# Where the first weight split of the next step stands in the vector queue of a fused encoder block on Trainium2

## The chip, the cores and the metric

The kernel is one program on one core of one Trainium2 chip. Its time is device microseconds (us) from one execution; the time before is the median of three runs. All five engines of the core take part: TensorE (PE) multiplies, ScalarE (ACT) rounds and evaluates functions, VectorE (DVE) subtracts, adds and multiplies, GpSimd (POOL) and SyncE (SP) mostly issue transfers. Each engine works through its own queue in the order in which the program was built.

## The reference

One encoder block on 256 tokens of width 4096, all in float32. Cut to its matrix products:

```python
h = rms_norm(x, pre_norm_gain)
proj = h @ w_in                      # 4096 x 24,704 columns
(q, k, v, gate_a, qi, ki, wi, z, xs, bm, cm, dt_raw, merge_logits) = split(proj)
y_a = dsa_attention(rope(q), rope(k), v, rope(qi), rope(ki), wi * s) * silu(gate_a)
y_b = ssd_mixer(xs, z, bm, cm, dt_raw, ...)
merged = (sigmoid(merge_logits)[0] * (y_a @ w_branch_attn)
          + sigmoid(merge_logits)[1] * (y_b @ w_branch_ssd))
out = merged @ w_out
return x + rms_norm(out, post_norm_gain)
```

The products with `w_in`, the two branch matrices and `w_out` are nearly all of the work. The attention (top 64 keys by an indexer, softmax) and the state-space scan are small beside them.

## The kernel before

**Precision.** A float32 operand is used as a sum of two parts: a rounded one ("h", fp32r) and the remainder ("l"). A product a·b is three matmuls, l(a)·h(b), h(a)·l(b) and h(a)·h(b), into one bank of PSUM. For the activations (256 tokens, kept in SBUF as `base` and as sums and differences `ext`) the two parts are made once. The weights are streamed from HBM and split as they arrive: `split` (line 483) takes one tile of two 128x512 blocks, lets ScalarE round it into a tile `wh` (line 486), and lets VectorE subtract to get the remainder `wl` (line 490, or line 488 where the sign is turned). Below, "rounding" and "remainder" mean these two instructions, and "a split" means both. In a matmul the activation part is the loaded weight matrix and the `wh` or `wl` block streams through.

**Two kinds of step.** Most products go through `pair_gemm` (line 515). It makes 256 tokens x 1024 columns at a time. Its loop runs over 16 pairs of row blocks of the weights (`plan`); each pair is a 2x2 block product and is one step. A step of kind S has 7 block products instead of 8, that is 21 matmuls, and pays with extra sums of weight blocks on VectorE (lines 598 and 599). A step of kind D or R has 8 block products, 24 matmuls. The program has 172 steps of kind S and 276 of kinds D and R, and every S step here is followed by a step of kind D or R.

**What a step of kind S puts on the engines**, in the order of the code (lines 593 to 605, kind "S"): the split of the second raw tile `rb`, the split of the first raw tile `ra`, the subtraction of line 598 in `ra`, the subtraction of line 599 in `rb`, the split of one block of `ra` (128x512, called t2 below), and the split of `rb` (t3 and t4, the last split of the step). Then its seven products in the order 2, 5, 3, 1, 6, 7, 4. The remainder of the last split is first read by the second matmul of product 7, which is matmul 17 of the 21. A step of kind D or R has two splits: first `ra` with the sign turned (rounding on line 486, remainder on line 488), read by its first 12 matmuls, then `rb`, read by its other 12.

**Buffers.** The rounded tiles lie in a pool of `SBUFS = 5` buffers, the remainders in another five. In both programs the first rounding of a step that follows an S step goes into the buffer of the last rounding before that S step, that is of the tile `rb` of the step ahead of it. It can be written when the last matmul of that earlier step has read it. Raw tiles have 8 buffers and are fetched two steps ahead (`LEAD = 2`).

**Order.** The program is written against a framework that reorders each engine's instructions by its own estimate of when each is ready, keeps the dependences, and adds the waits. Between the matmuls of a step, `step()` lets pending work (rotary embedding, softmax, the scan, evacuation of results) put out some instructions of its own; this is called side work below.

Of the kernel before, what the change touches and what calls it, by code (L numbers as in the profile page):

```python
# [19 lines left out]
S = 256  # L20
# [26 lines left out]
def fused_block(tc, x, xT, w_qi, w_misc, w_q0, w_qk, w_vg, w_x, w_z, w_gate, w_br, w_out2, w_out,  # L47
# [24 lines left out]
    def fbit(ap):  # L72
        return ap.bitcast(F32)
# [406 lines left out]
        k = int(name[2]) - 1  # L480
        return base[i][:, 0, k, tk], base[i][:, 1, k, tk]

    def split(src, n, sign=1):
        h = whp.tile([P, n, NW], F32R, tag="wh", name="wh")
        l = wlp.tile([P, n, NW], F32R, tag="wl", name="wl")
        A.activation(h, src, AF.Copy, scale=float(sign))  # L486
        if sign < 0:
            V.scalar_tensor_tensor(l, src, -1.0, fbit(h), ALU.mult, ALU.subtract)  # L488
        else:
            V.tensor_sub(l, src, fbit(h))  # L490
        return [(h[:, j, :], l[:, j, :]) for j in range(n)]
# [23 lines left out]
    def pair_gemm(what, mode, chunk, plan, outs, evac, hooks={}, pace=1):  # L515

        while len(live) > 1:
            drain(live.popleft())
        left = {}
        for _, kind in plan:  # L520
            for j, n in USES[kind].items():
                left[j] = left.get(j, 0) + n
        ps = {}
        dest = []

        def product(j, i, name, w):
            (ah, al), (bh, bl) = form(i, name), w
            first = j not in ps
            if first:
                ps[j] = bank(phys[j])  # L530
            left[j] -= 1
            for n, (l, r) in enumerate(((al, bh), (ah, bl), (ah, bh))):
                T.matmul(ps[j], l, r, start=first and n == 0, stop=left[j] == 0 and n == 2)  # L533

        def early():
            dest.extend(outs())
            A.activation(dest[0], ps[1], AF.Copy)
            V.tensor_add(dest[1], ps[6], dest[0])
            V.tensor_add(dest[2], ps[7], dest[1])

        def late():
            if not dest:
                dest.extend(outs())
                A.activation(dest[1], ps[5], AF.Copy, scale=-1.0)
                return
            V.tensor_add(dest[1], ps[5], dest[1])
            if 8 in ended:
                V.tensor_sub(dest[3], dest[3], ps[5])  # L548
                return
            V.scalar_tensor_tensor(dest[3], ps[5], -1.0, dest[2], ALU.mult, ALU.subtract)  # L550

        def rest():
            c11, c12, c21, c22 = dest
            if 1 not in ps:
                A.activation(c11, ps[2], AF.Copy)
                A.activation(c21, ps[4], AF.Copy)
                V.tensor_sub(c22, c12, ps[8])
                V.tensor_sub(c12, c12, ps[3])
                return
            V.scalar_tensor_tensor(c12, ps[3], -1.0, c12, ALU.mult, ALU.subtract)  # L560
            if 8 in ps and 8 not in ended:
                V.tensor_sub(c22, c22, ps[8])
            V.tensor_add(c11, ps[2], c11)
            V.tensor_add(c21, ps[4], c21)

        def end():
            rest()
            live.append(push(evac(dest)))

        after = max([n for n, (_, kind) in enumerate(plan) if kind == "S"], default=-2) + 1  # L570
        ended = []
        loaded = deque()

        def fetch(n):
            i, kind = plan[n]
            ra, rb = raw_tile(), raw_tile()
            load_half(ra, chunk(i), 0)
            load_half(rb, chunk(i), 1)
            if kind == "S":
                nc.gpsimd.dma_start(ra[:, 0, :], chunk(i)[:, HK, :], accum_op=ALU.add)  # L580
            loaded.append((ra, rb))

        for n in range(LEAD):
            fetch(n)
        for n, (i, kind) in enumerate(plan):
            if n + LEAD < len(plan):
                fetch(n + LEAD)
            ra, rb = loaded.popleft()
            if n in hooks:
                hooks[n]()  # L590
            assert kind_of[i] == what, (n, i, kind_of, len(aux))
            assert kind == "R" or ext_n[i] == {"S": 4, "D": 2}[kind], (n, i, ext_n)
            if kind == "S":
                b11, b21 = split(rb, 2)
                t1, b22 = split(ra, 2)
                if n == 1:
                    run_pending()
                V.tensor_sub(ra[:, 1, :], ra[:, 0, :], ra[:, 1, :])  # L598
                V.tensor_sub(rb, rb, ra[:, 1:2, :].to_broadcast([P, 2, NW]))  # L599
                t2, = split(ra[:, 1:2, :], 1)  # L600
                t3, t4 = split(rb, 2)
                now = {1: ("A11", b11), 2: ("A12", b21), 3: ("S4", b22), 4: ("A22", t4),
                       5: ("S1", t1), 6: ("S2", t2), 7: ("S3", t3)}
                for j in (2, 5, 3, 1, 6, 7, 4):
                    product(j, i, *now[j])
            else:
                w = {}
                w[1, 2], w[2, 2] = split(ra, 2, -1)
                w[1, 1], w[2, 1] = split(rb, 2)
                if n == 0 and len(pending) > 1 and turned[0] == "aux":  # L610
                    pending.pop(0)()
                if n == 1:
                    run_pending()
                if n == after:
                    early()
                    if not left.get(5):
                        late()
                        ended.append(5)
                if n == len(plan) - 1 and dest and not ended and left.get(8) == 0:
                    V.scalar_tensor_tensor(dest[3], dest[2], -1.0, ps[8], ALU.mult, ALU.subtract)  # L620
                    ended.append(8)
                todo = [(k, j) for j in ((5, 3, 2, 4) if kind == "D" else (3, 8, 2, 4))
                        for k in (1, 2)]
                for k, j in todo:
                    name = {2: f"A1{k}", 4: f"A2{k}", 8: f"A2{k}", 5: f"A2{k}",
                            3: f"D{k}" if kind == "D" else f"A1{k}"}[j]
                    product(j, i, name, w[k, 1 if j in (2, 4) else 2])
                    if (k, j) == todo[3]:
                        step(pace)
            step(pace)  # L630
        if 5 not in ended:
            pending.append(late)
        pending.append(end)
        turn(mode)
# [388 lines left out]
    for g, cols in enumerate(GATES):  # L1023
        last = g == len(GATES) - 1
        plan = kinds(SX if g > 1 else SS, range(16), range(8, 16) if last else ())
# [71 lines left out]
    for n in range(0, 8, 2):  # L1097
        for br in range(2):
            pairs = range(8 * br, 8 * br + 8)
            plain = pairs if (n, br) in ((0, 0), (6, 1)) else ()  # L1100
            plan = kinds(SY, pairs, plain)
# [47 lines left out]
    for n in range(0, 6, 2):  # L1149
# [5 lines left out]
        plan = [(i, "R" if k == "D" else k) for i, k in kinds(SM, order, plain)]  # L1155
# [65 lines left out]
    def finish_tok(t, ps):  # L1221
        with tc.high_priority():
# [7 lines left out]
         plan=[(h, (0, 1)) for h in range(12)]  # L1230
# [102 lines left out]
```

## Time and profile before

| | before |
|---|---|
| median of three runs | 2837.47 us (2835.63 to 2841.07) |
| the profiled execution | 2835.93 us |
| its span, first to last instruction | 2833.8 us |
| TensorE busy, matmuls | 2808.8 us (99%), 12744 |
| VectorE busy | 2318.9 us (82%) |
| ScalarE busy | 1693.3 us (60%) |
| mean granted TensorE clock | 0.998 |
| HBM traffic | 224 GB/s over the span |

In a row of the timeline view stand the start, the duration, the engine, the line of the kernel, the operation, its tiles written as out<-in (buffer numbers left out), the shape, how many equal instructions were merged into the row, and in brackets the idle time before it and what ended that. `b` and `ext` are activation parts, `p` and `pc` results. A matmul row with `wh` streams a rounded weight block, one with `wl` a remainder. The shown duration of a matmul is longer than its distance to the next one, since they overlap in the array. In the waits view a row has the total, the count and the longest wait in us. In a row of the groups view stand after the bar the busy time, the mean ns of one, and the idle time before.

### The profile page before, as it was taken

What the parts mean: (1) busy time and instruction counts of PE and PEld (TensorE: products, weight loads), DVE (VectorE), ACT (ScalarE), POOL (GpSimd) and SP (SyncE); (2) the same over time, 40 slices, a digit from 0 to 9 for tenths busy, and PEclk for the clock granted to TensorE, in tenths of its full rate; (3) what the DMA queues carried; (4) which work ended last, traced back from release to release, by engine and by line L of the source; (5) the groups of instructions that cost most, each with busy time, mean ns of one, the idle gap of its engine ahead of it and who ended that gap; (6) DMA issues with size and microseconds to landing.
All of it is one profiled execution on the core that took longest, in us unless ns stands there. A gap on an engine that the chain in (4) does not pass through costs nothing.

```text
span 2833.8 us, 36254 instructions
## 1 busy us (share of the span) xinstructions
PE 2808.8 (99%) x12744; PEld 2314.6 (82%) x12744; DVE 2318.9 (82%) x2867; ACT 1693.3 (60%) x2210; POOL 179.8 (6%) x216
## 2 busy tenths in 40 slices
PE   9999999999999999999999999999999999999998
PEld 7877888888888888888888888888887888888886
DVE  6668988888888878888888888888887889878875
ACT  7444565565656656886678755555565545555553
POOL 0100000000000000000000000000000000000000
PEclk9999999999999999999999999999999999999999
DMA  9544776777767776666666877877777887877883
GB/s 373 192 159 165 214 222 202 226 212 222 223 200 224 212 220 217 195 201 207 209 192 195 256 245 242 247 231 244 236 242 243 245 259 242 284 226 227 257 259 134
DMA packets 198696, 637.54 MB, mean 225 GB/s; under 512 B 22385, under 2 KB 23153, under 8 KB 198513
## 3 DMA queue, kind: packets, MB, share of 16 engines
q1 hardware_dynamic: 163728, 567.05, 59.8%
q0 software_dynamic: 27008, 52.44, 10.5%
q10 hardware_dynamic: 7776, 15.73, 1.5%
q8 instruction: 100, 1.64, 0.2%
q14 instruction: 84, 0.68, 0.1%
HBM read 615.21 MB, written 19.92 MB: 224 GB/s over the span
## 4 chain that ended last, share of the span: by engine, by line
PE 89%; DVE 5%; issue 3%; DMA 2%; ACT 1%; SPq 0%; POOL 0%; DVEq 0%; ACTq 0%; POOLq 0%
PE p L533 74%; PE p L193 4%; PE p L194 4%; PE p L195 4%; DVE wl L490 1%; PE p L363 1%; ACT wh L486 1%; DMA fr<-yscr 1%; PE p L890 0%; DVE raw L599 0%; DMA raw<-w_x_d 0%; DVE wl L185 0%; PE p L758 0%; PE p L725 0%; PE p L394 0%
## 5 line engine op out<-in xcount | busy, mean ns | idle before, releaser
L486 ACT ACTIVATE wh<-raw 128x1024 fp32r<-128x1024 f32 (+1 forms) x1240 | 1190.9, 995 | 775.3 <-PE p L533 443.0
L533 PE MATMUL p<-wh,b 128*128 128x512 f32 x4504 | 1511.9, 393 | 3.5 <-DVE pc L548 1.9
L490 DVE TENSOR_TENSOR wl<-raw,wh 128x1024 fp32r<-128x1024 f32 (+1 forms) x964 | 1064.1, 1125 | 242.8 <-ACT wh L486 237.7
L533 PEld LDWEIGHTS p<-wh,b 128*128 128x128 f32 x4504 | 846.5, 188 | 179.3 <-ACT wh L486 4.4
L533 PE MATMUL p<-wl,b 128*128 128x512 f32 x2252 | 878.8, 390 | 1.6 <-DVE wl L490 0.9
L533 PE MATMUL p<-wh,ext 128*128 128x512 f32 x2320 | 810.4, 390 | 0.0
L533 PEld LDWEIGHTS p<-wh,ext 128*128 128x128 f32 x2320 | 435.5, 188 | 91.2 <-ACT wh L486 0.9
L533 PEld LDWEIGHTS p<-wl,b 128*128 128x128 f32 x2252 | 423.5, 188 | 88.2 <-DVE wl L488 2.7
L533 PE MATMUL p<-wl,ext 128*128 128x512 f32 x1160 | 452.6, 390 | 0.6 <-DVE wl L490 0.2
L488 DVE SCALAR_TENSOR_TENSOR wl<-raw,wh 128x1024 fp32r<-128x1024 f32 x276 | 337.0, 1221 | 86.5 <-ACT wh L486 82.5
L533 PEld LDWEIGHTS p<-wl,ext 128*128 128x128 f32 x1160 | 217.8, 188 | 48.5 <-DVE wl L490 2.8
L599 DVE TENSOR_TENSOR raw<-raw 128x1024 f32<-128x1024 f32 x172 | 210.5, 1224 | 4.2
L185 DVE TENSOR_TENSOR wl<-raw,wh 128x1024 fp32r<-128x1024 f32 x112 | 138.7, 1240 | 84.4 <-ACT wh L184 84.3
L193 PE MATMUL p<-wh,b 128*128 128x512 f32 x512 | 201.4, 394 | 1.4 <-ACT wh L181 1.4
L194 PE MATMUL p<-wl,b 128*128 128x512 f32 x512 | 199.6, 390 | 0.2 <-DVE wl L182 0.2
L195 PE MATMUL p<-wh,b 128*128 128x512 f32 x512 | 199.3, 389 | 0.0
L184 ACT ACTIVATE wh<-raw 128x1024 fp32r<-128x1024 f32 x112 | 118.2, 1059 | 130.3 <-PE p L195 117.0
L598 DVE TENSOR_TENSOR raw<-raw 128x512 f32<-128x512 f32 x172 | 118.6, 689 | 3.8
L193 PEld LDWEIGHTS p<-wh,b 128*128 128x128 f32 x512 | 96.0, 188 | 25.9 <-ACT wh L181 3.4
L194 PEld LDWEIGHTS p<-wl,b 128*128 128x128 f32 x512 | 96.2, 188 | 20.2 <-DVE wl L182 1.0
L195 PEld LDWEIGHTS p<-wh,b 128*128 128x128 f32 x512 | 96.1, 188 | 20.1
L580 POOL DMA_DIRECT2D raw<-w_gate_d x50 | 43.3, 867 | 587.5 <-DMA raw<-w_gate_d 280.2
(238 smaller groups left out, 1443.4 us busy)
## 6 DMA issues: line engine op xcount, KB each, us to landing
raw<-w_gate_d SPq DMA_DIRECT2D x256, 512.0 KB, 5.1
raw<-w_vg_d SPq DMA_DIRECT2D x128, 512.0 KB, 4.8
raw<-w_x_d SPq DMA_DIRECT2D x128, 512.0 KB, 4.7
raw<-w_br_d SPq DMA_DIRECT2D x128, 512.0 KB, 4.8
raw<-w_out_d SPq DMA_DIRECT2D x128, 512.0 KB, 4.8
raw<-w_qk_d SPq DMA_DIRECT2D x96, 512.0 KB, 4.7
raw<-w_z_d SPq DMA_DIRECT2D x64, 512.0 KB, 4.8
raw<-w_qi_d SPq DMA_DIRECT2D x62, 512.0 KB, 5.5
```

Of the source, the lines that this page charges most:

```text
L184: A.activation(wh, rs, AF.Copy)
L185: V.tensor_sub(wl, rs, wh.bitcast(F32))
L193: T.matmul(ps[t], al[:, tk], wh[:, i, :], start=first, stop=False)
L194: T.matmul(ps[t], ah[:, tk], wl[:, i, :], start=False, stop=False)
L195: T.matmul(ps[t], ah[:, tk], wh[:, i, :], start=False, stop=last)
L486: A.activation(h, src, AF.Copy, scale=float(sign))
L488: V.scalar_tensor_tensor(l, src, -1.0, fbit(h), ALU.mult, ALU.subtract)
L490: V.tensor_sub(l, src, fbit(h))
L533: T.matmul(ps[j], l, r, start=first and n == 0, stop=left[j] == 0 and n == 2)
L580: nc.gpsimd.dma_start(ra[:, 0, :], chunk(i)[:, HK, :], accum_op=ALU.add)
L598: V.tensor_sub(ra[:, 1, :], ra[:, 0, :], ra[:, 1, :])
L599: V.tensor_sub(rb, rb, ra[:, 1:2, :].to_broadcast([P, 2, NW]))
```

## The change

`split` gets a function `between`, which it calls after it has put out the rounding and before it puts out the remainder. The first split of a step is moved into `head(n)`. The last split of an S step calls `head(n + 1)` in between; in a step that does not follow an S step, `head(n)` is called at the start of the step. No instruction is added or dropped by this; the first split of a step after an S step is built earlier, and the last remainder of the S step is built after both its instructions.

```diff
-    def split(src, n, sign=1):
+    def split(src, n, sign=1, between=None):
         h = whp.tile([P, n, NW], F32R, tag="wh", name="wh")
         l = wlp.tile([P, n, NW], F32R, tag="wl", name="wl")
         A.activation(h, src, AF.Copy, scale=float(sign))
+        if between is not None:
+            between()
         if sign < 0:
             V.scalar_tensor_tensor(l, src, -1.0, fbit(h), ALU.mult, ALU.subtract)
         else:
...
+        heads = {}
+
+        def head(n):
+            if n < len(plan) and n not in heads:
+                ra, rb = loaded[0]
+                heads[n] = split(rb, 2) if plan[n][1] == "S" else split(ra, 2, -1)
+
...
         for n, (i, kind) in enumerate(plan):
             if n + LEAD < len(plan):
                 fetch(n + LEAD)
+            head(n)
             ra, rb = loaded.popleft()
...
             if kind == "S":
-                b11, b21 = split(rb, 2)
+                b11, b21 = heads[n]
                 t1, b22 = split(ra, 2)
...
                 t2, = split(ra[:, 1:2, :], 1)
-                t3, t4 = split(rb, 2)
+                t3, t4 = split(rb, 2, between=lambda: head(n + 1))
...
             else:
                 w = {}
-                w[1, 2], w[2, 2] = split(ra, 2, -1)
+                w[1, 2], w[2, 2] = heads[n]
                 w[1, 1], w[2, 1] = split(rb, 2)
```

A line of the old program stands two to ten lines lower in the new one: the remainders are on lines 488 and 490 before and on 490 and 492 after, the matmul on 533 and 535, the two subtractions on 598 and 599 and on 608 and 609.

VectorE's queue of the program before, in the S step at 1707 us of the profiled execution. The tile wl_14860 is the remainder of t2, wl_14864 that of the last split of the step, wl_14889 the first and wl_14893 the second remainder of the step that follows.

```order
L598 TENSOR_TENSOR raw_14769<-raw_14769 128x512
L599 TENSOR_TENSOR raw_14770<-raw_14770,raw_14769 128x1024
L490 TENSOR_TENSOR wl_14860<-raw_14769,wh_14859 128x512
L490 TENSOR_TENSOR wl_14864<-raw_14770,wh_14863 128x1024
L488 SCALAR_TENSOR_TENSOR wl_14889<-raw_14813,wh_14888 128x1024
L490 TENSOR_TENSOR wl_14893<-raw_14814,wh_14892 128x1024
```

The same place in the changed program; the first remainder of the following step is now wl_14867.

```order
L608 TENSOR_TENSOR raw_14769<-raw_14769 128x512
L609 TENSOR_TENSOR raw_14770<-raw_14770,raw_14769 128x1024
L492 TENSOR_TENSOR wl_14860<-raw_14769,wh_14859 128x512
L490 SCALAR_TENSOR_TENSOR wl_14867<-raw_14817,wh_14866 128x1024
L492 TENSOR_TENSOR wl_14864<-raw_14770,wh_14863 128x1024
L492 TENSOR_TENSOR wl_14893<-raw_14818,wh_14892 128x1024
```

The two remainders have changed places: the following step's first one stands ahead of the S step's last one. It is so in all 172 S steps. ScalarE's queue has the three roundings in the same order in both programs.

On TensorE the framework keeps the order of the matmuls around most S steps and changes it around some. The next piece is from before, in the S step at 1724 us; wh_15000 and wl_15001 are its last split (products 7 and 4), wh_15036 and wl_15037 the first split of the step after it.

```order
L533 MATMUL p4_15021<-wh_15000,ext_2525 128x512
L533 MATMUL p4_15021<-wl_15001,ext_2525 128x512
L533 MATMUL p4_15021<-wh_15000,ext_2525 128x512
L533 MATMUL p6_14969<-wh_15000,b1_79 128x512
L533 MATMUL p6_14969<-wl_15001,b1_79 128x512
L533 MATMUL p6_14969<-wh_15000,b1_79 128x512
L533 MATMUL p1_14948<-wh_15036,b2_80 128x512
L533 MATMUL p1_14948<-wl_15037,b2_80 128x512
L533 MATMUL p1_14948<-wh_15036,b2_80 128x512 x2
```

The same place in the changed program, where the step's last split is still wh_15000 and wl_15001 and the following one is wh_15003 and wl_15004.

```order
L535 MATMUL p4_15025<-wh_15000,ext_2525 128x512
L535 MATMUL p6_14969<-wh_15000,b1_79 128x512
L535 MATMUL p1_14948<-wh_15003,b2_80 128x512
L535 MATMUL p1_14948<-wl_15004,b2_80 128x512
L535 MATMUL p1_14948<-wh_15003,b2_80 128x512 x2
L535 MATMUL p4_15025<-wl_15001,ext_2525 128x512
L535 MATMUL p4_15025<-wh_15000,ext_2525 128x512
L535 MATMUL p6_14969<-wl_15001,b1_79 128x512
L535 MATMUL p6_14969<-wh_15000,b1_79 128x512
```

Here five matmuls that do not need wl_15001 have been moved ahead of the first one that does. Counted over the program, the first reader of an S step's last remainder is matmul 17 of the step in 162 of 172 S steps before and in 108 after; in the other 64 between one and nineteen other matmuls stand ahead of it. GpSimd's queue is unchanged, and in SyncE's some weight loads and loads of the gates have changed places by a few positions.

## The prediction

> **What bounds the kernel now.** I read the page first: who is busy, and who is on the chain that ended last.
>
> ```profile
> PE 2808.8 (99%) x12744; PEld 2314.6 (82%) x12744; DVE 2318.9 (82%) x2867; ACT 1693.3 (60%) x2210; POOL 179.8 (6%) x216
> PE 89%; DVE 5%; issue 3%; DMA 2%; ACT 1%; SPq 0%; POOL 0%; DVEq 0%; ACTq 0%; POOLq 0%
> ```
>
> TensorE is busy throughout and carries 89% of the chain. Next come the waits: first those of TensorE in the pair products, then the largest of ScalarE.
>
> ```profile
> PE p L533 <- ACT wh L486: 1.6, 5, 0.5
> PE p L533 <- DVE wl L490: 1.2, 2, 0.9
> PE p L533 <- DVE wl L488: 0.5, 1, 0.5
> ACT wh L486 <- PE p L533: 443.0, 358, 2.6
> ```
>
> TensorE waits for splits 3.3 us in all (1.6 + 1.2 + 0.5), while ScalarE waits for TensorE to free buffers 358 times. The splits run ahead of the matmuls and are held back by the five buffers. So the change can gain hardly anything, and the question is whether it lets a remainder come too late. For that I read the timeline of one ordinary S step, engine by engine. TensorE:
>
> ```profile
> 1706.77 0.39 PE L533 MATMUL p<-wh,b 128*128 128x512 f32 x1
> ...
> 1709.27 0.62 PE L533 MATMUL p<-wh,b 128*128 128x512 f32 x2
> ...
> 1712.66 0.62 PE L533 MATMUL p<-wh,ext 128*128 128x512 f32 x2
> 1713.12 0.39 PE L533 MATMUL p<-wl,ext 128*128 128x512 f32 x1
> 1713.35 0.39 PE L533 MATMUL p<-wh,ext 128*128 128x512 f32 x1
> ```
>
> At 1706.77 the earlier step begins the 12 matmuls on its second split. The first of the two in the row at 1709.27 is the twelfth, the other begins the S step. The row at 1713.12 is matmul 17 of the S step, the first reader of its last remainder. From 1706.77 to 1713.12 are 28 matmuls, 0.227 us each: nothing waits. ScalarE and then VectorE in the same step:
>
> ```profile
> 1707.01 0.63 ACT L486 ACTIVATE wh<-raw 128x512 fp32r<-128x512 f32 x1 [2.48 <-PE p L533]
> 1708.27 1.06 ACT L486 ACTIVATE wh<-raw 128x1024 fp32r<-128x1024 f32 x1 [0.63 <-DVE raw L599]
> 1709.74 1.06 ACT L486 ACTIVATE wh<-raw 128x1024 fp32r<-128x1024 f32 x1 [0.41 <-PE p L533]
> ```
>
> ```profile
> 1702.67 3.50 DVE L490 TENSOR_TENSOR wl<-raw,wh 128x1024 fp32r<-128x1024 f32 x3 [0.81 <-ACT wh L486]
> ...
> 1708.07 0.68 DVE L490 TENSOR_TENSOR wl<-raw,wh 128x512 fp32r<-128x512 f32 x1
> 1709.37 1.22 DVE L490 TENSOR_TENSOR wl<-raw,wh 128x1024 fp32r<-128x1024 f32 x1 [0.61 <-ACT wh L486]
> 1710.84 1.23 DVE L488 SCALAR_TENSOR_TENSOR wl<-raw,wh 128x1024 fp32r<-128x1024 f32 x1 [0.24 <-ACT wh L486]
> ```
>
> The rounding of the last split (1708.27) is early. The next step's first rounding (1709.74) is the one that waits for TensorE: its buffer is free only when the twelfth matmul (1709.27 + 0.39 = 1709.66) has read it. Before the change the last remainder (1709.37) does not care; it ends at 1710.59, 2.53 us ahead of its reader at 1713.12.
>
> **The change, part by part.** No instruction is added. On ScalarE the two roundings keep their order and, here, their times. On VectorE the two remainders change places, and that adds a wait: the last remainder of the S step now stands behind the next step's first one, which waits for a rounding that waits for the matmuls of the step before. VectorE's 0.61 us of idling is not filled but lengthened; what is queued behind is the last remainder, and TensorE waits for that.
>
> *An ordinary S step.* The next step's first remainder stays at 1710.84. The last one follows it directly. Three remainders in a row took 3.50 us (row at 1702.67), so at 1.22 us each they start (3.50 - 1.22) / 2 = 1.14 us apart. The last remainder starts at 1711.98 and ends at 1713.20 instead of 1710.59. Counted from the start of the rounding that was held, the end comes 1713.20 - 1709.74 = 3.46 us later, and TensorE's reader is due 1713.12 - 1709.74 = 3.38 us later. It is late by a hair, and what a wait costs TensorE is seen where it already waits for this very remainder:
>
> ```profile
> 2430.72 1.22 DVE L490 TENSOR_TENSOR wl<-raw,wh 128x1024 fp32r<-128x1024 f32 x1
> ```
>
> ```profile
> 2431.26 0.61 PE L533 MATMUL p<-wh,ext 128*128 128x512 f32 x2
> 2432.00 0.50 PE L533 MATMUL p<-wl,ext 128*128 128x512 f32 x1
> 2432.34 0.40 PE L533 MATMUL p<-wh,ext 128*128 128x512 f32 x1
> ...
> 2433.49 0.39 PE L533 MATMUL p<-wl,b 128*128 128x512 f32 x1
> ```
>
> The remainder ends at 2431.94 and the matmul starts 0.06 us after it. Then the next matmul comes after 0.34 us instead of 0.227, and the six from 2432.00 to 2433.49 take 1.49 us instead of 1.36: a restart costs 0.13 us beside the delay. So an ordinary step loses 3.46 + 0.05 - 3.38 = 0.13 us of delay and 0.13 us of restart, 0.26 us together. Nothing gives it back: the next S step's chain starts again from its own twelfth matmul, which has moved along.
>
> The Trainium skill bears on the 1.14 us: "VectorE: DVE Perf Modes", section "The DRAIN you can't avoid", has the next VectorE instruction start only when the pipe of the one before is empty. By that the last remainder would start 0.08 us later and each ordinary step would lose 0.34 us; the row of three in 3.50 us shows starts 0.08 us inside the one before, and I go by the row.
>
> *How many.* I went through all 172 S steps in the timeline and the order. In 108 the reader is still matmul 17. In 102 of these the next step's first rounding waits for TensorE, as above. In 80 of the 102 the reader is due 3.37 to 3.43 us after that rounding starts; in 22 side work among the matmuls gives it 0.13 us or more beyond what it needs. The first and the last of the 80, the rounding and the reader of each:
>
> ```profile
> 345.16 1.06 ACT L486 ACTIVATE wh<-raw 128x1024 fp32r<-128x1024 f32 x1 [1.66 <-PE p L533]
> ```
>
> ```profile
> 348.54 0.39 PE L533 MATMUL p<-wl,ext 128*128 128x512 f32 x1
> ```
>
> ```profile
> 2722.95 1.06 ACT L486 ACTIVATE wh<-raw 128x1024 fp32r<-128x1024 f32 x1 [0.41 <-PE p L533]
> ```
>
> ```profile
> 2726.32 0.39 PE L533 MATMUL p<-wl,ext 128*128 128x512 f32 x1
> ```
>
> The distances are 3.38 and 3.37 us. Term one: 80 x 0.26 = 20.8 us. Its bounds: 80 x 0.13 = 10.4 us if a short wait has no restart, and nothing if the distance were 0.13 us better than I reckon.
>
> *Where ScalarE and VectorE are behind already.* In 12 steps the splits are late for reasons of their own, and moving the last remainder back one place makes it late by 0.01 to 1.7 us. The first clear one (ScalarE, VectorE, and the reader on TensorE):
>
> ```profile
> 319.79 4.86 ACT L486 ACTIVATE wh<-raw 128x1024 fp32r<-128x1024 f32 x5 [0.62 <-DVE raw L599]
> ```
>
> ```profile
> 320.88 1.23 DVE L490 TENSOR_TENSOR wl<-raw,wh 128x1024 fp32r<-128x1024 f32 x1 [0.61 <-ACT wh L486]
> 322.02 1.22 DVE L488 SCALAR_TENSOR_TENSOR wl<-raw,wh 128x1024 fp32r<-128x1024 f32 x1
> ```
>
> ```profile
> 322.70 0.39 PE L533 MATMUL p<-wl,ext 128*128 128x512 f32 x1
> ```
>
> The second of the five roundings ends near 319.79 + 0.95 + 1.06 = 321.80, so the next step's remainder runs from 321.84 and the last one from 322.98 to 324.20; its reader was due at 322.70 and starts at 324.25, 1.55 us late. Reckoned alike, the 12 come to 9.5 us; three of them, between 306 and 328 us, follow each other, and one delay serves them all, which leaves 7.7 us. Ten restarts add 1.3. Term two: 9.0 us, with bounds of 0 (the splits make the time up elsewhere) and 11 us.
>
> *The 64 steps with a new order on TensorE.* There other matmuls, on the next step's first split, fill the time ahead of the late reader, and that split is ready first now. I take 0 beyond the few already in term two. If that cover failed they would lose 0.26 us each, 16.6 us.
>
> *The rest.* The order of three roundings on ScalarE, GpSimd's queue and the fetches into raw tiles keep their places; a raw tile is released up to 2.6 us later with two steps (some 10 us) in hand. I take 0.
>
> Sum: 20.8 + 9.0 = 29.8 us on 2835.93, 2865.7 us. That execution lies 1.5 us below the median of the three runs and inside their range, so I say 2866 us.
>
> **The rivals.**
>
> *A short wait costs only its delay.* The matmul that waits is the first after a row of others; if the next weight load is taken ahead while it waits, there is no restart. Then term one is 10.4 and term two 7.7, and the time is 2836 + 18 = 2854 us. Against it speaks the row at 2432.34. The Trainium skill speaks for it: "TensorE: Matmul & The Clock Gate", section "Architectural detail: the array is 16× 32×32, not 1× 128×128", says TensorE's queue can pull weight loads ahead of matmuls in flight. By that rule the step would lose 0.13 us; the trace agrees where nothing waits (0.23 us from 1713.12 to 1713.35), not behind a wait (0.34 us).
>
> *The remainder is just in time.* The whole of term one hangs on 0.08 us of lateness and 0.05 us of signal. If the remainder came 0.13 us sooner, TensorE would not notice, and only about half of term two would be left: 2835.9 + 4.5 = 2840 us. That the distance is the same in 80 steps speaks against it.
>
> *Not slower: the early split pays.* The next step's first remainder is ready up to 1.14 us sooner where the engines are behind, and takes away TensorE's waits for splits there. They are 3.3 us in 8 waits (5 + 2 + 1), with 8 restarts of 0.13 us 4.3 us, which gives 2835.9 - 4.3 = 2832 us. It decides only if an ordinary step loses less than 4.3 / 80 = 0.05 us.
>
> *The side work makes it worse.* In the new order side work on VectorE stands in the gap ahead of the two remainders in 66 of the 172 steps, and in the scan stage it waits for TensorE and ScalarE itself. If that doubled term two and opened the cover of a third of the 64 steps, 9 + 5.5 us more: 2880 us.
>
> **How the numbers follow.** Forecast 0.65, delay only 0.17, just in time 0.07, early split pays 0.02, side work 0.09. A measurement of this kernel can tell about 0.2%, 5.7 us. Of these only "just in time" lies within that, and only "early split pays" below: faster 0.02, same 0.07, slower 0.91. The range leaves out those two and the edges of the others: its low end, 2846 us, is term one without restarts and term two at nothing (2835.9 + 10.4); its high end, 2884 us, the side work's 2880 with term two doubled from its bound of 11 us instead of 9.
>
> **What would show it.** In the changed profile: TensorE's waits for VectorE's remainders rise from 3 to about 80 short ones; matmul 17 of ordinary S steps starts 0.13 us late and the next one 0.34 us after it; line 492 starts 1.14 us after line 490 in S steps and waits for nothing; the idle time ahead of line 490's first remainder grows. I am wrong if matmul 17 keeps its distance of 3.38 us from the held rounding, or if that rounding no longer waits for TensorE.

## The result and the profile after

| | before | after |
|---|---|---|
| median | 2836.55 us (2834.54 to 2841.07, 4 runs) | 2870.02 us (2867.15 to 2871.65, 4 runs) |
| profiled execution | 2835.93 us | 2869.7 us |
| its span | 2833.8 us | 2867.9 us |
| mean granted TensorE clock | 0.998 | 0.997 |

The changed kernel is slower: the ratio is 1.0115, with a 95% interval of 1.0097 to 1.0132. The forecast was 2866 us. The spans differ by 34.1 us, and it is these that are taken apart below.

The first two lines of the page of after, the busy time of each engine and the chain that ended last:

```profile
PE 2836.5 (99%) x12744; PEld 2307.6 (80%) x12744; DVE 2298.7 (80%) x2867; ACT 1693.6 (59%) x2208; POOL 179.7 (6%) x216
PE 88%; DVE 6%; issue 3%; ACT 2%; DMA 1%; POOL 0%; SPq 0%; DVEq 0%; ACTq 0%; POOLq 0%
```

They hide the loss: TensorE is still "99% busy", with 28 us more of busy time for the same 12744 matmuls, because the shown duration of a matmul overlaps the next one and stretches over a short wait (0.50 us instead of 0.39 at 1735.79 below). The waits tell more, and the same waits must be read on two engines. First TensorE's matmuls, then its weight loads:

```profile
PE p L535 <- DVE wl L492: 5.7, 6, 1.7
...
PE p L535 <- DVE wl L490: 2.0, 4, 1.0
```

```profile
PEld p L535 <- DVE wl L492: 41.8, 94, 2.1
PEld p L535 <- DVE wl L490: 5.7, 12, 1.3
```

In the kernel before, the weight loads' waits for the remainders were few:

```profile
PEld p L533 <- DVE wl L490: 4.1, 7, 1.3
PEld p L533 <- DVE wl L488: 2.7, 7, 1.0
```

Among the matmuls 6 waits for the remainder of line 492 are seen, among the weight loads 94. From the starts themselves, the first reader of an S step's last remainder starts within 0.075 us of that remainder's end in 88 steps of after and in 4 of before. All 88 are among the 94 waits of the weight loads; only 3 of them are among the 6 of the matmuls, whose other 3 are for other remainders.

VectorE's wait has moved as the order of its queue says. In the groups view, the idle time (after the second bar) stood ahead of the remainders without a turned sign and now stands ahead of the next step's first one. Before, then after:

```profile
L490 DVE TENSOR_TENSOR wl<-raw,wh 128x1024 fp32r<-128x1024 f32 (+1 forms) x964 | 1064.1, 1125 | 242.8 <-ACT wh L486 237.7
...
L488 DVE SCALAR_TENSOR_TENSOR wl<-raw,wh 128x1024 fp32r<-128x1024 f32 x276 | 337.0, 1221 | 86.5 <-ACT wh L486 82.5
```

```profile
L492 DVE TENSOR_TENSOR wl<-raw,wh 128x1024 fp32r<-128x1024 f32 (+1 forms) x964 | 1049.9, 1123 | 36.8 <-ACT wh L486 35.0
...
L490 DVE SCALAR_TENSOR_TENSOR wl<-raw,wh 128x1024 fp32r<-128x1024 f32 x276 | 337.1, 1221 | 329.9 <-ACT wh L486 329.9
```

The ordinary S step that the prediction followed (reader at 1713.12 us before) reads like this in after: ScalarE, VectorE, TensorE's matmuls and its weight loads.

```profile
1730.78 1.06 ACT L486 ACTIVATE wh<-raw 128x1024 fp32r<-128x1024 f32 x1 [0.63 <-DVE raw L609]
1732.29 1.06 ACT L486 ACTIVATE wh<-raw 128x1024 fp32r<-128x1024 f32 x1 [0.44 <-PE p L535]
```

```profile
1733.38 1.22 DVE L490 SCALAR_TENSOR_TENSOR wl<-raw,wh 128x1024 fp32r<-128x1024 f32 x1 [2.11 <-ACT wh L486]
1734.52 2.35 DVE L492 TENSOR_TENSOR wl<-raw,wh 128x1024 fp32r<-128x1024 f32 x2
```

```profile
1735.21 0.61 PE L535 MATMUL p<-wh,ext 128*128 128x512 f32 x2
1735.79 0.50 PE L535 MATMUL p<-wl,ext 128*128 128x512 f32 x1
1736.13 0.39 PE L535 MATMUL p<-wh,ext 128*128 128x512 f32 x1
1736.36 0.40 PE L535 MATMUL p<-wh,b 128*128 128x512 f32 x1
```

```profile
1735.79 0.19 PEld L535 LDWEIGHTS p<-wl,ext 128*128 128x128 f32 x1 [0.39 <-DVE wl L492]
1735.90 0.19 PEld L535 LDWEIGHTS p<-wh,ext 128*128 128x128 f32 x1
```

The last split is rounded by 1731.84, but its remainder starts only at 1734.52, 1.14 us after the next step's first one (1733.38), which waited 2.11 us for the rounding that TensorE held until 1732.29. It ends at 1734.52 + 1.22 = 1735.74, and matmul 17 starts at 1735.79: 3.50 us after the held rounding instead of 3.38, so it is 0.12 us late. The next matmul comes 0.34 us behind it (1736.13), and then the old distance of 0.23 is back. The row of the weight load shows what the restart is. Where nothing waits, a load runs 0.23 us ahead of its matmul (the load at 1735.90 belongs to the matmul at 1736.13). The load for matmul 17 holds an activation part that has long been ready, and yet it waits for the remainder with its matmul and starts in the same moment, 1735.79, so that its time is no longer hidden. The trace says why: no matmul of this program has a wait of its own. All waits of the matrix products stand in weight loads (in 2715 of the 12744 in after), so a load is held by whatever its matmul has to wait for. In all 88 late readers load and matmul start within 0.002 us of each other.

To see where the 34.1 us are, the time from the first matmul of one S step to the first matmul of the next was compared between the two traces, and the steps were sorted as the prediction sorted them. The 58 are its 64 reordered steps without those that it counted among the 12:

| S steps | forecast, us | measured, us |
|---|---|---|
| 80 ordinary | 20.8 | 21.1 (median step 0.266) |
| 12 where the splits are late already | 9.0 | 4.3 |
| 58 reordered: 20 in the scan stage | 0 | 10.2 |
| 58 reordered: 38 elsewhere | 0 | -1.2 |
| 22 with time to spare | 0 | 0.2 |
| ahead of the first S step | 0 | -0.5 |

The "scan stage" is here the stretch of eight column tiles from the first z tile to the second gate tile, 49 S steps, 917 to 1643 us before and 923 to 1665 us after; all of its S steps together lost 15.2 us.

Each figure compares one trace of each kernel, and two of them must be read with care. The -1.2 us is no gain of the change: one stretch, behind the S step at 2075 us, is 2.07 us shorter in after, and there the trace of before has the granted clock at half for 3.4 us (at 2142 us) and that of after does not. The other 37 steps lost 0.9 us. And some 2 of the 10.2 us are a drop of the clock in a single step, told in the last section.

### The profile page after: what moved, and what is told of

It reads as the page before. It is cut to its first block, busy times and chain, and to the rows that moved or that the text cites. A ratio compares the mean times of both kernels' runs of the same rounds, so it can differ in the third digit from the quotient of the medians.

```text
span 2867.9 us, 36370 instructions
## 1 busy us (share of the span) xinstructions
PE 2836.5 (99%) x12744; PEld 2307.6 (80%) x12744; DVE 2298.7 (80%) x2867; ACT 1693.6 (59%) x2208; POOL 179.7 (6%) x216
## 4 chain that ended last, share of the span: by engine, by line
PE 88%; DVE 6%; issue 3%; ACT 2%; DMA 1%; POOL 0%; SPq 0%; DVEq 0%; ACTq 0%; POOLq 0%
PE p L535 75%; PE p L193 3%; PE p L194 3%; PE p L195 3%; DVE wl L492 1%; DVE wl L185 1%; ACT wh L486 1%; PE p L363 1%; DMA fr<-yscr 1%; DVE raw L609 0%; DVE cacc L836 0%; PE p L900 0%; PE p L768 0%; PE p L735 0%; PE p L394 0%
## 5 line engine op out<-in xcount | busy, mean ns | idle before, releaser
L492 DVE TENSOR_TENSOR wl<-raw,wh 128x1024 fp32r<-128x1024 f32 (+1 forms) x964 | 1049.9, 1123 | 36.8 <-ACT wh L486 35.0
L490 DVE SCALAR_TENSOR_TENSOR wl<-raw,wh 128x1024 fp32r<-128x1024 f32 x276 | 337.1, 1221 | 329.9 <-ACT wh L486 329.9
L535 PE MATMUL p<-wl,ext 128*128 128x512 f32 x1160 | 460.7, 399 | 4.7 <-DVE wl L492 4.7
```

## The experiments

The theory: the loss of an ordinary step is nothing but the lateness of the first reader of the last remainder, plus a restart of TensorE. The rivals: rounding earlier costs something of its own; a short wait has no restart; or the new order as such costs, wherever the reader stands. Every ratio below is against the kernel before on the same chip (medians there 2837.68, 2837.99 and 2834.13 us for the three chips used); the microseconds of the groups of steps come from each run's own trace, against the trace of before.

**1. Only the rounding goes in between.** The next step's first rounding stays where the change puts it, its remainder goes back behind the last one.

```diff
         A.activation(h, src, AF.Copy, scale=float(sign))
-        if between is not None:
-            between()
+        second = between() if between is not None else None
...
             V.tensor_sub(l, src, fbit(h))
+        if second is not None:
+            second()
```

> The changed kernel with only the rounding of the next step's first split in between; its remainder stands behind the S step's last remainder again, as before the change. My theory (all of the loss is in VectorE's order): 2833 to 2840 us, and TensorE waits for remainders as rarely as before. Rival (the rounding that ScalarE's queue holds earlier keeps its side work back, or the framework's new order does): 2845 us or more.

Measured: 2836.62 us (11 runs), ratio 0.9995 (0.9987 to 1.0004). The 80 ordinary steps lost 0.0 us, the scan stage 0.1. VectorE in the same ordinary step:

```profile
1711.53 1.23 DVE L491 TENSOR_TENSOR wl<-raw,wh 128x1024 fp32r<-128x1024 f32 x1 [0.61 <-ACT wh L486]
1713.00 1.23 DVE L503 SCALAR_TENSOR_TENSOR wl<-raw,wh 128x1024 fp32r<-128x1024 f32 x1 [0.24 <-ACT wh L499]
```

The two idle times are again 0.61 and 0.24 us, as before the change. So all of the loss comes with the order of the two remainders on VectorE. What the framework sets anew around them goes back with it: the reader is matmul 17 in 162 steps again, as before the change.

**2. A reader one matmul later.** The change is kept; product 7 puts its third matmul ahead of the second, so that the remainder is first read by matmul 18.

```diff
-            for n, (l, r) in enumerate(((al, bh), (ah, bl), (ah, bh))):
+            three = ((al, bh), (ah, bl), (ah, bh))
+            if j == 7:
+                three = ((al, bh), (ah, bh), (ah, bl))
+            for n, (l, r) in enumerate(three):
```

> The changed kernel with the last two matmuls of product 7 exchanged, so that the first reader of the last remainder is matmul 18 in most steps, 0.23 us later; the remainder then ends 0.15 us before it. My theory, with the restart put down to the weight load that is held with its matmul (it begins about 0.2 us ahead of it): the delay of 0.13 us goes and a part of the restart stays, 10 to 21 us less than the changed kernel, 2849 to 2860 us. If the matmul alone were held: no cost left in ordinary steps, 2849 us. If lateness were not the cause: 2868 to 2872 us.

Measured: 2852.22 us, ratio 1.0052 (1.0039 to 1.0064). The ordinary steps lost 2.3 us in place of 21.1. VectorE, the matmuls and the weight loads:

```profile
1723.55 1.23 DVE L490 SCALAR_TENSOR_TENSOR wl<-raw,wh 128x1024 fp32r<-128x1024 f32 x1 [1.88 <-ACT wh L486]
1724.69 2.36 DVE L492 TENSOR_TENSOR wl<-raw,wh 128x1024 fp32r<-128x1024 f32 x2
```

```profile
1725.38 0.84 PE L538 MATMUL p<-wh,ext 128*128 128x512 f32 x3
1726.06 0.40 PE L538 MATMUL p<-wl,ext 128*128 128x512 f32 x1
1726.30 0.39 PE L538 MATMUL p<-wh,b 128*128 128x512 f32 x1
```

```profile
1725.96 0.19 PEld L538 LDWEIGHTS p<-wl,ext 128*128 128x128 f32 x1 [0.16 <-DVE wl L492]
1726.07 0.19 PEld L538 LDWEIGHTS p<-wh,b 128*128 128x128 f32 x1
```

The remainder ends at 1725.91 and the reader starts at 1726.06, 0.15 us later. The weight load still waits 0.16 us for it, but it starts 0.10 us ahead of its matmul, and the matmuls keep 0.23 to 0.24 us. A lateness of 0.03 us is left in each ordinary step, and of the restart nearly nothing.

**3. The last remainder in two halves.** The remainder of the last split is made by two instructions of 128x512; the reader of matmul 17 needs only the first.

```diff
+        elif between is not None:
+            for j in range(n):
+                V.tensor_sub(l[:, j, :], src[:, j, :], fbit(h[:, j, :]))
         else:
             V.tensor_sub(l, src, fbit(h))
```

> The changed kernel with the S step's last remainder made by two instructions, t3's block first. Product 7 reads t3 alone, whose half is ready about 0.5 us sooner than the whole; t4's half comes as late as the whole did, but its reader is matmul 20. My theory: the 21 us of ordinary steps go, 2845 to 2851 us. Rivals that do not rest on the lateness of this remainder: 2868 to 2875 us, the more for 172 more instructions.

Measured: 2852.13 us, 1 us above the expected range, ratio 1.0049 (1.0036 to 1.0062). The reader stays matmul 17, and the ordinary steps lost 0.1 us.

```profile
1722.85 1.23 DVE L490 SCALAR_TENSOR_TENSOR wl<-raw,wh 128x1024 fp32r<-128x1024 f32 x1 [1.77 <-ACT wh L486]
1723.99 1.29 DVE L493 TENSOR_TENSOR wl<-raw,wh 128x512 fp32r<-128x512 f32 x2
```

The first half ends 0.46 us ahead of the reader, and the loss is gone with the reader at its old place on TensorE.

**4. A reader three matmuls later.** The change is kept; products 7 and 4 first issue the two matmuls of each on the rounded part, then the two on the remainder.

```diff
-                for j in (2, 5, 3, 1, 6, 7, 4):
+                for j in (2, 5, 3, 1, 6):
                     product(j, i, *now[j])
+                for j in (7, 4):
+                    product(j, i, *now[j], (0, 2), 1)
+                for j in (7, 4):
+                    product(j, i, *now[j], (1,), 1)
```

> The changed kernel with the two matmuls that read the last remainder (of products 7 and 4) put last, so that its first reader is matmul 20 or later, 0.68 us after the place of matmul 17. My theory: the remainder ends 0.6 us ahead, neither delay nor restart is left in ordinary steps, and some of the later-than-ordinary steps are covered too: 2842 to 2849 us. Rivals not resting on this remainder: 2868 to 2872 us.

Measured: 2850.38 us, also above the expected range, ratio 1.0045 (1.0033 to 1.0057); the ordinary steps lost 0.1 us, with 0.60 us from the remainder's end to its reader. Runs 2 to 4 together: the loss of the 80 steps is 21.1, 2.3, 0.1 and 0.1 us where the remainder (or the half that is read) ends 0.06, 0.15, 0.46 and 0.60 us ahead of the reader. In these steps lateness is all of it. But all three kernels stay 12 to 15 us slower than before, and by the steps 9 to 11 us of that lie in the scan stage. That was not expected. In runs 2 and 4 a stretch at half the granted clock near 1290 us, 3.4 and 6.8 us long, is part of it; run 3 has none there and still lost 9.3 us in the stage.

**5 and 6. The change in the scan stage alone, and everywhere else.** A flag is set ahead of the first z tile and taken back behind the second gate tile.

```diff
-                t3, t4 = split(rb, 2, between=lambda: head(n + 1))
+                t3, t4 = split(rb, 2, between=(lambda: head(n + 1)) if here[0] else None)
```

> The change is applied only from the first z projection through the second gate product, the stage with the scan's side work, 49 S steps of 172. By the place of the loss in the profile of the changed kernel this stage holds 15 us of the 34 (19 ordinary steps with 5 us, the rest where VectorE and ScalarE are behind): 2849 to 2854 us. If the loss outside depended on the stage or the reverse, the two parts would not add up to 34 us.

> The change is applied everywhere but in the stage with the scan's side work, 123 S steps of 172. By the place of the loss in the profile of the changed kernel, 19 us of the 34 lie here, 16 of them in 61 ordinary steps: 2853 to 2858 us.

Measured: 2852.98 us, ratio 1.0053 (1.0041 to 1.0065), for the scan stage alone; 2857.2 us, ratio 1.0066 (1.0054 to 1.0078), for all the rest. 15.0 and 19.2 us add up to 34.2, as much as the spans of the whole change differ by, so neither part hangs on the other. In the first, the scan stage lost 13.2 us, of which its 19 ordinary steps 4.8 and its 20 reordered ones 8.0; the granted clock does not drop in the stage there, so these 8.0 us are without it. In the second, the 61 ordinary steps outside it lost 16.2.

**7 and 8. A sixth rounded buffer.** With it the next step's first rounding does not wait for the twelfth matmul. It fits only with seven raw tiles instead of eight, so the kernel before was given the same.

```diff
-RBUFS = 8
+RBUFS = 7
...
-    whp = root(tc.tile_pool(name="whp", bufs=SBUFS))
+    whp = root(tc.tile_pool(name="whp", bufs=SBUFS + 1))
```

> The changed kernel with 6 buffers for rounded tiles instead of 5, and 7 for raw tiles instead of 8 to make room. My theory (the last remainder is late because it stands behind a rounding that waits for TensorE to free the fifth buffer): with a sixth buffer the held rounding starts some 2.7 us sooner in ordinary S steps, matmul 17 waits nowhere in them, and the 21 us of the 80 ordinary steps go; 2840 to 2850 us. Rival (the new order of matmuls and of side work costs the time, whatever the buffers): 2865 to 2872 us.

> Control: the kernel before with 6 buffers for rounded tiles and 7 for raw tiles. Its splits run ahead already and TensorE waits 3.3 us for them: within 0.2% of before, 2832 to 2841 us. If fewer raw tiles cost anything, it shows here and not as a part of the change.

Measured: the change with six buffers 2877.2 us, ratio 1.0134 (1.0119 to 1.015); the kernel before with six 2858.88 us, ratio 1.0069 (1.0057 to 1.0081). Both expectations on the total missed. The part that the theory speaks of came: the ordinary steps of the changed kernel lost 1.0 us instead of 21.1, with the remainder ending 1.3 to 2.5 us ahead of the reader in 72 of them and 0.1 to 1.1 us in the other 8. What came on top came without the change too: the control lost 27.9 us in the scan stage. ScalarE waits longer there for the weights to arrive, which fits the missing raw tile, though the two buffer changes were not tried apart. In the kernel before and then in the control:

```profile
ACT wh L486 <- DMA raw<-w_x_d: 3.5, 1, 3.5
```

```profile
ACT wh L486 <- DMA raw<-w_x_d: 16.4, 4, 6.2
...
ACT wh L486 <- DMA raw<-w_gate_d: 12.0, 5, 5.6
```

The clock is another part: in that stage the trace of the control has 20.4 us at half the granted clock, that of the change with six buffers 27.2 us, and that of before none. These two kernels therefore say little on the change's total. Why the change with six buffers is 18 us slower than its control, with the ordinary loss gone, is left open; the clock can make up at most 5 us of it (30.6 us at half in its whole trace short of the end, against 20.4).

**9 and 10. Both cures at once.** The change everywhere but in the scan stage (5 and 6, the flag the other way round) with the reader at matmul 20 (4); and the matmul order of 4 alone in the kernel before.

> The changed kernel with both cures measured so far: the change is made everywhere but in the scan stage, and the matmuls of products 7 and 4 on the last split's remainder are issued last, so that the first reader is matmul 20. Theory (outside the scan stage the loss is the lateness of that reader and nothing else): the 19 us of the change outside the scan stage go, down to the few us that stay in the steps that are behind for other reasons (4 us with reader 20); 2837 to 2842 us, within 0.2% of the kernel before. Rival (the two cures overlap, or the swap of the two remainders costs something of its own): 2845 us or more.

> The kernel before with only the order of the matmuls changed: products 7 and 4 issue their matmuls on the remainder last (reader 20 instead of 17). Control for the runs with reader 20. Theory: before, the last remainder is 2.5 us early in an ordinary step, so there is nothing to gain there; of the few late steps some 1 to 4 us: 2833 to 2838 us. If the exchange itself costs something (another order of the accumulating matmuls, weight parts loaded twice), 2840 to 2845 us, and so much of what stayed in the run with reader 20 is not the change's.

Measured: 2835.28 us (11 runs), 2 us below the expected range, ratio 1.0006 (0.9997 to 1.0015); and 2833.64 us (11 runs), ratio 0.9996 (0.9987 to 1.0005). With the reader out of the way and the scan stage left alone the change costs nothing that can be measured, and it gains nothing either. The later reader has no price and no gain of its own.

**11 and 12. Less side work ahead of the splits in the scan stage.** The change in the scan stage alone, with the three last pieces of an S step issued at high priority there; and the same in the kernel before (with `split(rb, 2)` in the last line).

```diff
                 V.tensor_sub(ra[:, 1, :], ra[:, 0, :], ra[:, 1, :])
-                V.tensor_sub(rb, rb, ra[:, 1:2, :].to_broadcast([P, 2, NW]))
-                t2, = split(ra[:, 1:2, :], 1)
-                t3, t4 = split(rb, 2, between=(lambda: head(n + 1)) if here[0] else None)
+                with (tc.high_priority() if here[0] else nullcontext()):
+                    V.tensor_sub(rb, rb, ra[:, 1:2, :].to_broadcast([P, 2, NW]))
+                    t2, = split(ra[:, 1:2, :], 1)
+                    t3, t4 = split(rb, 2, between=(lambda: head(n + 1)) if here[0] else None)
```

> The change in the scan stage alone, and there the subtraction in rb, the split of t2 and the last split with the next step's first one are put out with high priority, so that the framework lets less side work of VectorE stand ahead of t2's remainder (22 instructions instead of 59 between the first subtraction and t2's remainder, over the 49 S steps). Theory (the scan stage loses because the swapped remainders and the side work that the framework puts around them push the later splits back): of the 13 us of the scan stage about half comes back, 2842 to 2848 us. Rival (the scan stage loses only at the reader of the last remainder): as with the change in the scan stage alone, 2850 to 2855 us.

> Control for the run with priority in the scan stage: the kernel before with the same three pieces of the S steps of the scan stage put out with high priority (26 side instructions instead of 61 ahead of t2's remainder), the remainders in their old order. Theory: the waits of the scan stage before are 2 to 3 us, so 2833 to 2839 us; if side work that is pushed back comes late for its own readers, 2840 to 2845 us, and the comparison above must be made against this run.

Measured: 2839.39 us (11 runs), ratio 1.0016 (1.0008 to 1.0025), where the scan stage alone had 1.0053; the control 2833.87 us (11 runs), ratio 0.9996 (0.9988 to 1.0005). More came back than expected: the 20 reordered steps of the stage lost -0.4 us instead of 8.0, while the 19 ordinary steps kept their loss (5.2 us, 0.27 each). So the stage loses in two ways: the late reader in its ordinary steps, and in the others, most likely, the place that side work takes among VectorE's and ScalarE's instructions. The run does not hold all else equal: in 11 of the 20 fewer matmuls stand ahead of the late reader than in run 5. Against a price of the new order of matmuls as such stand the 38 reordered steps outside the stage, which lost next to nothing. The weight loads' waits in the scan stage, with the change in that stage alone (919 to 1658 us of it) and then with priority (915 to 1646):

```profile
PEld p L536 <- DVE wl L492: 11.3, 25, 1.6
PEld p L536 <- ACT wh L486: 9.4, 20, 0.7
PEld p L536 <- DVE wl L490: 3.3, 6, 1.0
```

```profile
PEld p L537 <- DVE wl L493: 9.7, 27, 0.7
PEld p L537 <- ACT wh L487: 4.5, 9, 0.8
PEld p L537 <- DVE wl L491: 2.1, 5, 1.0
```

The waits for VectorE's plain remainders keep their number but not their length (1.6 to 0.7 us at most), and those for the roundings halve. Which pieces of side work do the harm is not settled: in the order of VectorE's instructions the change alone raises the side work between t2's remainder and the last remainder from 49 to 108 instructions over the 49 S steps, and priority leaves it there (115), cutting instead what stands ahead of t2's remainder (59 to 22).

One step shows how such a place looks. It is the costliest single one, 4.7 us, at 1557 us before and 1570 us after. VectorE before, then after:

```profile
1555.83 0.68 DVE L598 TENSOR_TENSOR raw<-raw 128x512 f32<-128x512 f32 x1
1556.55 1.23 DVE L599 TENSOR_TENSOR raw<-raw 128x1024 f32<-128x1024 f32 x1
1557.69 0.69 DVE L490 TENSOR_TENSOR wl<-raw,wh 128x512 fp32r<-128x512 f32 x1
...
1564.10 0.69 DVE L661 TENSOR_TENSOR fr<-b 128x512 f32<-128x512 f32 x1
```

```profile
1572.23 0.68 DVE L608 TENSOR_TENSOR raw<-raw 128x512 f32<-128x512 f32 x1
1573.46 0.69 DVE L671 TENSOR_TENSOR fr<-b 128x512 f32<-128x512 f32 x1 [0.55 <-PE p L915]
1574.07 1.22 DVE L609 TENSOR_TENSOR raw<-raw 128x1024 f32<-128x1024 f32 x1
1575.21 0.68 DVE L492 TENSOR_TENSOR wl<-raw,wh 128x512 fp32r<-128x512 f32 x1
```

The side work of line 671 (661 before), which waits for TensorE, stood behind the whole step and now stands between its two subtractions. The second one starts 1.84 us after the first instead of 0.72, and t2's remainder with it. TensorE in after:

```profile
1575.95 0.50 PE L535 MATMUL p<-wl,ext 128*128 128x512 f32 x1 [1.10 <-DVE wl L492]
```

It waits 1.10 us for t2's remainder, a reader that the prediction did not look at. In run 5 the same step lost 2.6 us; what is added to that in after is told in the last section.

## Why the prediction was right, and where it was not

**What bounds the kernel, and where the wait goes: right.** The two remainders change places, VectorE's idle time goes ahead of the next step's first one (86.5 to 329.9 us in its group), and the last remainder comes late. Run 1 shows that the earlier rounding costs nothing: with the remainders in their old order the time is that of the kernel before.

**Term one: right, and for its reason.** 80 steps by 0.26 us was 20.8 us; measured 21.1, with 0.12 us of delay and 0.11 of a weight load that is no longer hidden in the step shown, 0.266 us as the median. Runs 2 to 4 take the delay away in three ways, and the loss goes with it. The row of three remainders gave the start of the last one rightly: it starts 1.14 us after the one ahead of it, 0.08 inside that one's 1.22. The 0.34 us a step that the prediction drew from the Trainium skill's section "The DRAIN you can't avoid" ("VectorE: DVE Perf Modes") do not show. The prediction took half of what stands there: the section goes on that a next instruction that is not held starts earlier, and the rows, 1.14 us apart with 1.22 us shown, agree with that.

**"Delay only" fell** by the restart: 0.34 us to the next matmul in after. The Trainium skill's "Architectural detail: the array is 16× 32×32, not 1× 128×128" ("TensorE: Matmul & The Clock Gate") says that TensorE's queue can pull weight loads ahead of matmuls in flight. The trace agrees for the matmuls behind the reader, whose loads run 0.23 us ahead. At the reader it does not speak against it, as the prediction thought: there the wait for the remainder stands in the load itself. What the step would lose if the wait stood in the matmul, no run here shows. **"Just in time"** was nearer than its chance of 0.07 says: run 2 differs from the changed kernel by one matmul of 0.23 us, and 19 of 21 us are gone. **"The early split pays"** fell: run 9, which lets the next step's remainder come early at no price elsewhere, gained nothing. Its 3.3 us in 8 waits were read on the matmuls alone; the weight loads of the same trace wait 12.1 us for splits in 26 waits (5.3, 4.1 and 2.7 us), so the rival's price was read too low, though a load's wait is in part hidden by its lead of 0.23 us.

**Term two: its size was off.** The steps named lost 4.3 us, not 9.0. Two of them carry it: the one at 306 us lost 1.96 and the one at 2428 us lost 2.32, each more than the 1.7 us of delay that the prediction gave as the most for any. The other ten together lost nothing: the step at 319 us, reckoned 1.55 us late, lost 0.26, which fits the prediction's remark that one delay serves three steps there, and the one at 1502 us lost nothing. Of these ten two were 0.7 and 0.6 us shorter than before, at 657 and 832 us; they were so in run 11 too, which has no change there, so that is not the change's.

**The 64 reordered steps: this step failed.** The prediction took 0, because the matmuls moved ahead of the reader cover it. The cover held for that reader: outside the scan stage 37 of these 38 steps lost 0.9 us together. In the scan stage they lost 10.2 us, some 2 of them by a drop of the clock in one step and most of the others at other readers: over the stage, the distances into the first readers of t2's split grew by 3.4 us and into those of the next step's two splits by 3.5. The prediction had looked at the order of TensorE and of the splits there and at the side work ahead of the two exchanged remainders, not at what the framework sets anew around t2's split and the splits of the following step. Its rival "the side work makes it worse", at 0.09 and 14.5 us beside the forecast, named the likely cause but another road: there the side work doubled term two and uncovered the reader of the last remainder, and neither happened. So the sum came near (29.8 for 34.1 us) with two errors of opposite sign, 4.7 too much and 9.0 too little, and that part of it is luck.

**What would show it.** Matmul 17 is 0.12 us late, the next one 0.34 behind, the last remainder starts 1.14 us after the one ahead of it and waits for nothing: all as written. The "about 80 short waits" are there, but not on the engine that was named: TensorE's matmuls show 6, its weight loads 94.

## What to carry to other kernels

In a queue that runs in order, a piece that waits for something late must not stand ahead of a piece that is ready and has a reader at a fixed distance: here 2.5 us of slack became 0.1 us of lateness, 80 times over. One matmul between the ready data and its reader was worth 19 us, so look at the slack of the reader before moving what feeds it. And where a scheduler sets the order of the side work, compare the order of the whole queue in each stage, not only of the pieces that the change names.

## What the runs showed of the hardware

**A short wait of TensorE is seen on the weight loads.** Of 88 late readers the matmuls' waits show 3 and the weight loads' all 88, since a matmul is shown with 0.39 us and follows the one ahead after 0.23; a wait of 0.1 us does not open a gap. The weight load starts 0.23 us ahead in a full row, so its idle time shows it (0.39 us in the step above).

**How late is late.** A remainder that ended 0.15 us ahead of its reader cost 0.03 us in a step, one that ended 0.46 us ahead nothing, one that the reader had to wait for 0.27 us. The step from 0.03 to 0.27 lies within one matmul.

**The clock fell to half in a single step.** In the step at 1570 us of after, behind the waits shown above, the granted clock is 0.50 for 6.8 us. Three stretches of that trace, then the same place in run 5, with the granted clock as the number after the last busy time in brackets:

```profile
1566.00:1576.00 10.00, 8.63 (x40) 6.47 (x38) 9.45 (x17) 8.78 (x13) 0.00 (x0) 1.00 0.38 126
1576.80:1583.60 6.80, 6.64 (x15) 4.24 (x14) 5.87 (x12) 6.77 (x14) 0.86 (x1) 0.50 0.61 177
1584.00:1592.00 8.00, 8.00 (x41) 6.71 (x40) 5.70 (x7) 4.39 (x6) 0.00 (x0) 1.00 0.98 331
```

```profile
1555.00:1590.00 35.00, 32.75 (x147) 25.60 (x146) 31.86 (x48) 31.12 (x46) 0.86 (x1) 1.00 0.67 220
```

In the slow stretch matmuls follow each other after 0.43 us. By the clock alone that would be an estimated 6.8 x (1 - 0.50) = 3.4 us. But runs 2 to 5, which have the change at this step and no drop there, lost 2.4, 2.7, 2.2 and 2.6 us in it, so the drop adds only 2.0 to 2.5 of the 4.7 us; why not all 3.4 is not shown. Such drops stand in other traces too, always to 0.50 and, short of the end of the trace, 3.4, 6.8 or 10.2 us long; in before there is one of 3.4 us at 2142 us. That the waits ahead of it brought the clock down was not tried; in runs 2 to 5, with their losses of 2.2 to 2.7 us at this step, the clock stayed at 1.00.
